# A hybrid attention layer: gates as one silu in place on ScalarE, multiplied in on GpSimd chunk by chunk

## The chip, the cores and the metric

One core of a Trainium2 chip runs one launch of the kernel. The metric is device time in microseconds, the median of several executions. TensorE is called PE below, VectorE DVE, ScalarE ACT, GpSimd POOL; SP issues most DMAs.

## The reference

One decoder layer with 512 tokens and a model width of 1024, in f32. The input is normalized and projected to queries, keys, values and gates of two attentions with 8 heads of 64 each: sliding-window attention (window 128, with sinks) and block attention (a query sees its own block of 256, causally, and the past one). Each attention's output is multiplied by silu(gate) before the output projection; a gated per-layer embedding and a last norm follow.

```python
a_out = swa_attention(a_q, a_k, a_v, sinks, rel_bias[:, :8])
b_out = moba_attention(b_q, b_k, b_v, rel_bias[:, 8:])
mixed = jnp.concatenate([a_out * jax.nn.silu(a_g), b_out * jax.nn.silu(b_g)], axis=-1)
x = x + mixed @ w_out
gate = jax.nn.sigmoid(rms_norm(x, ple_g) @ w_ple_gate)
return rms_norm(x + (p_i @ w_ple_proj) * gate, final_norm)
```

## The kernel before

Every f32 product on PE is made of three products of high and low halves, so a result that PE needs again is split: ACT copies it to the high half (`split_T`, L143) and DVE subtracts to get the low half (L144). Activations and gates lie transposed, as 8 chunks of 128 channels by 512 tokens: `O[c]` is attention output, `G[c]` the raw gate; chunks 0 to 3 belong to the window attention, 4 to 7 to the block attention, two heads to a chunk.

The middle phase interleaves two things on PE, in an order written by hand. One is a stream of projection pieces (L451 to L453 and L137 to L139), whose results ACT and DVE evacuate: queries (`make_q`, L498, L499), keys (`make_k`, L143, L144, followed by a POOL DMA, L508), values, and raw gates (`raw_g`, L527; the last gate by DVE, L529). The other is attention steps. `swa_step(u)` runs 16 window steps: scores on PE (L551), DVE adds the bias and takes the row's minimum of the negated scores (L554), ACT takes the exponential with its row sum (L557), POOL folds two halves (L563), DVE normalizes by the reciprocal (L564, L566); one step later PE transposes the rows (L574), ACT and DVE split the transpose (`pta`, L143, L144), POOL masks it (L582); another step later PE multiplies by the values (L591), and ACT and DVE evacuate to `O` (L596, L601). `moba_step(m)` does the same for the block attention, 32 steps and 6 to drain: scores L611, reduction L612, exponential L614, normalization L617 to L621, transposes L631 (those of a head run while the next head's scores are taken, so they come some four steps after its exponentials), split `pt` (L143, L144), products with the values L641, one step after the transposes, evacuation L648, L649.

PE and SP keep the order of the program text (`manual_schedule`). On ACT, DVE and POOL a planner orders the instructions by its own estimates of when each can start, so an instruction can run earlier or later than where it is written. A wait for the engine's turn is then in order: what stands behind a waiting instruction on its engine waits too.

The gates: `silu_gate(c)` takes a temporary tile `sg` (two buffers of pool `xa`, shared with the evacuations' `aux`), ACT writes Sigmoid(G) (L534), DVE multiplies by G (L535), POOL multiplies O by it (L536). It is called for chunks 0 to 3 after the last window step, for 4 and 5 at step 33 of the block attention, for 6 and 7 at the split of `O` into `acts`, which feeds the output projection (L137 to L139 with `hi_wo`, `lo_wo`). Where an exponential follows a Sigmoid, or a Sigmoid an exponential, the built kernel has an ACT_TABLE_LOAD between them on ACT.

Of the kernel before, what the change touches and what calls it, by code (L numbers as in the profile page):

```python
# [10 lines left out]
F32 = mybir.dt.float32  # L11
BF16 = mybir.dt.bfloat16
F32R = mybir.dt.float32r
AF = mybir.ActivationFunctionType
ALU = mybir.AluOpType

P = 128
SEQ = 512
# [20 lines left out]
def hybrid_layer_kernel(  # L39
# [16 lines left out]
    nc = tc.nc  # L56
# [22 lines left out]
    def bank(shape, name, tag):  # L79
        return psum.tile(shape, F32, name=name, tag=tag)  # L80
# [60 lines left out]
    def split_T(hi, lo, src):  # L141

        nc.scalar.activation(hi, src, AF.Copy)  # L143
        nc.vector.tensor_sub(lo, src, hi.bitcast(F32))  # L144
# [241 lines left out]
    with ExitStack() as ph2:  # L386
        def pool(name, bufs):
            return ph2.enter_context(tc.tile_pool(name=name, bufs=bufs, reuse_waits="tile"))
# [8 lines left out]
        xa = pool("xa", 2)  # L397

        O = [op.tile([P, SEQ], F32, name=f"O_{c}") for c in range(8)]
        G = {}  # L400
# [3 lines left out]
        def toep(head, swa):  # L404

            if swa:
                b = bp.tile([P, 2, 256], F32, name="b_a", tag="b")
                src = bass.AP(tensor=d_tab.tensor, offset=d_tab.offset + head * JT + JB,
                              ap=[[1, P], [JT, 2], [1, 256]])
            else:  # L410
                b = bp.tile([P, 512], F32, name="b_b", tag="b")
                src = bass.AP(tensor=d_tab.tensor, offset=d_tab.offset + (HA + head) * JT,
                              ap=[[1, P], [1, 512]])
            nc.sync.dma_start(b, src)
            return b
# [16 lines left out]
        def run(n):  # L432
            while stream and (n > 0 or stream[0][0] == 0):
                c, f = stream.popleft()
                n -= c
                f()

        def run_all():
            while stream:
                stream.popleft()[1]()  # L440
# [89 lines left out]
            G[c] = g  # L530

        def silu_gate(c):
            sg = xa.tile([P, SEQ], F32, name="sg", tag="aux")
            nc.scalar.activation(sg, G[c], AF.Sigmoid)  # L534
            nc.vector.tensor_mul(sg, sg, G[c])  # L535
            nc.gpsimd.tensor_mul(O[c], O[c], sg)  # L536


        def swa_scores(c, i, q, kt, bias):
# [63 lines left out]
        def moba_scores(h, i, q, kt, bias):  # L603
            w = (i + 1) * P
            S = bank([P, 512], "Sb", "S")
            st = sp.tile([P, 520], F32, name="stb", tag="st")
            nm = small.tile([P, 1], F32, name="nmb")
            sm = small.tile([P, 1], F32, name="smb")
            ri = small.tile([P, 1], F32, name="rib")
            for j in range(2):  # L610
                nc.tensor.matmul(S[:, :w], q[:, i, :], kt[:, j, :w], start=j == 0, stop=j == 1)  # L611
            nc.vector.tensor_tensor_reduce(st[:, :w], S[:, :w], bias[:, 512 - w:], -1.0, 1.0e38,  # L612
                                           ALU.add, ALU.min, nm)
            nc.scalar.activation(st[:, :w], st[:, :w], AF.Exp, bias=nm, scale=-1.0, accum_out=sm)  # L614

            def norm():
                nc.vector.reciprocal(ri, sm)  # L617
                if i == 3:
                    nc.scalar.activation(st[:, :w], st[:, :w], AF.Copy, scale=ri)
                else:  # L620
                    nc.vector.tensor_scalar_mul(st[:, :w], st[:, :w], ri)  # L621
            return st, norm
# [3 lines left out]
        def moba_trans(g, sts):  # L626
            tp = bank([P, 512], "tpb", "tp")
            o = 0
            for j in GRP[g]:
                for i in range(j, NT):  # L630
                    nc.tensor.transpose(tp[:, o:o + P], sts[i][:, tok(j)], rev)  # L631
                    o += P
            pt = pp.tile([P, 2, 512], F32R, name="pt", tag="pt")
            return lambda: split_T(pt[:, 0, :o], pt[:, 1, :o], tp[:, :o]), pt

        def moba_av(h, g, pt, oacc):
            o = 0
            for j in GRP[g]:
                w = SEQ - j * P
                for l in range(2):  # L640
                    nc.tensor.matmul(oacc[:, j * P:], Vb[:, j, h].rearrange("p a d -> p (a d)"),  # L641
                                     pt[:, l, o:o + w], start=j == 0 and l == 0, stop=j == 3 and l == 1)
                o += w

        def moba_evac(h, oacc):
            c, s = 4 + h // 2, h % 2
            aux = xa.tile([DH, 512], F32, name="auxb", tag="aux")
            nc.scalar.activation(aux, oacc[DH:P, :], AF.Copy)  # L648
            nc.vector.tensor_add(O[c][s * DH:(s + 1) * DH, :], oacc[0:DH, :], aux)  # L649
# [97 lines left out]
        swa_step(16)  # L747
        swa_step(16)
        for c in range(4):
            silu_gate(c)  # L750
        run(12)


# [4 lines left out]
        def moba_step(m):  # L758
            h, i = divmod(m, 4)
            norm = None  # L760
            if h < HB:
                if i == 0 and h + 2 < HB:
                    bb[h + 2] = toep(h + 2, False)
                st, norm = moba_scores(h, i, qb[h // 2][h % 2], kb[h // 2][h % 2], bb[h])
                sts[h, i] = st
            pace(per * 0.4)
            if norm:
                norm()
            new = None
            if h > 0 and i > 0 and h - 1 < HB:  # L770
                sp_, pt = moba_trans(i - 1, [sts[h - 1, k] for k in range(NT)])
                sp_()
                new = (h - 1, i - 1, pt)
            pace(per * 0.4)
            if ptq:
                h2, g2, pt2 = ptq.popleft()
                if g2 == 0:
                    ob[h2] = bank([P, 512], "oaccb", "o")
                moba_av(h2, g2, pt2, ob[h2])
                if g2 == 2:  # L780
                    moba_evac(h2, ob[h2])
            if new:
                ptq.append(new)
            pace(per * 0.2)

        for m in range(32):
            moba_step(m)
        per = 2.0
        for m in range(32, 38):
            moba_step(m)  # L790
            if m == 33:
                for c in (4, 5):
                    silu_gate(c)
        run_all()

        for c in range(KC):
            if c >= 6:
                silu_gate(c)
            split_T(acts[:, c, 0, :], acts[:, c, 1, :], O[c])

# [190 lines left out]
```

## Time and profile before

| | |
|---|---|
| median of 3 runs | 323.25 us (322.18 to 323.43) |
| profiled execution | 322.3 us, span 320.6 us |
| PE busy | 307.7 us, 96% |
| DVE busy | 226.0 us, 70% |
| ACT busy | 185.9 us, 58% |
| POOL busy | 66.3 us, 21% |
| middle phase with attention | about 32 to 220 us |

Times in rows are counted from the span's start. A timeline row gives the start, the duration, the engine, the line and operation, the tiles, and in brackets the idle time of the engine before it with what ended it. PE's matmuls are pipelined, so their durations overlap.

### The profile page before, as it was taken

The page shows a single profiled execution, that of the slowest core. Times are in us where ns is not written, and L with a number is a line of the kernel's source. Part 1 is how long each engine was busy: PE and PEld are TensorE (multiplying, and loading weights), DVE is VectorE, ACT ScalarE, POOL GpSimd, SP SyncE. Part 2 cuts the span into 40 slices and gives each one's busy share as a digit, 9 for nine tenths or more (in the row PEclk, how much of TensorE's full clock was granted, in tenths as well). Part 3 has the DMA queues.
Part 4 walks back from the last instruction along what each step waited for, and adds up shares of the span by engine and source line. Part 5 has one row for each costly group of instructions (what it writes and reads, how often), then busy time and mean ns, then how long its engine had stood idle before and what let it go on. Part 6 is the DMA issues. An engine that isn't in the chain of part 4 may idle for free.

```text
span 320.6 us, 4721 instructions
## 1 busy us (share of the span) xinstructions
PE 307.7 (96%) x1641; PEld 259.9 (81%) x1641; DVE 226.0 (70%) x516; ACT 185.9 (58%) x419; POOL 66.3 (21%) x118
## 2 busy tenths in 40 slices
PE   7999999999999999899999999999999999999990
PEld 6878788888889888699888878877888888888890
DVE  2876766886787868878878796859758656672544
ACT  4755656656475648677678676788157323541341
POOL 1240102435434351600003130012300110000011
PEclk9999999999999999999999999999999999999997
DMA  7962598150405072751443403004956700000113
GB/s 234 390 164 83 148 227 232 41 133 1 127 7 177 23 183 76 200 155 40 135 98 120 112 0 133 1 0 116 384 174 246 264 1 0 2 0 0 66 67 131
DMA packets 33224, 37.61 MB, mean 117 GB/s; under 512 B 1432, under 2 KB 24992, under 8 KB 33200
## 3 DMA queue, kind: packets, MB, share of 16 engines
q1 hardware_dynamic: 31952, 33.94, 34.0%
q0 software_dynamic: 800, 2.62, 4.2%
q10 hardware_dynamic: 448, 0.74, 0.7%
q8 instruction: 13, 0.21, 0.3%
q14 instruction: 11, 0.09, 0.1%
HBM read 32.52 MB, written 2.16 MB: 108 GB/s over the span
## 4 chain that ended last, share of the span: by engine, by line
PE 72%; DVE 12%; issue 6%; ACT 4%; POOL 3%; DMA 1%; POOLq 0%; SPq 0%; ACTq 0%; DVEq 0%
PE acc L451 8%; PE acc L452 8%; PE acc L453 8%; PE acc L137 7%; PE acc L139 7%; PE acc L138 7%; PE acc_ple L283 3%; PE acc_akv L302 3%; PE Sb L611 3%; PE accv L137 2%; PE oaccb L641 2%; PE accv L139 2%; PE accv L138 2%; PE tpb L631 2%; DVE q L499 2%
## 5 line engine op out<-in xcount | busy, mean ns | idle before, releaser
L557 ACT ACTIVATE st<-st,nm 128x257 f32<-128x257 f32 (+1 forms) x32 | 15.2, 478 | 22.0 <-DVE nm L554 20.0
L137 PE MATMUL acc<-hi_wg,h 128*128 128x512 f32 (+1 forms) x72 | 26.7, 370 | 0.0
L139 PE MATMUL acc<-hi_wg,h 128*128 128x512 f32 (+1 forms) x72 | 26.4, 367 | 0.0
L451 PE MATMUL acc<-acts,hi_bkq 128*128 128x512 f32 x64 | 26.4, 412 | 0.0
L138 PE MATMUL acc<-lo_wg,h 128*128 128x512 f32 (+1 forms) x72 | 26.3, 365 | 0.0
L451 PE MATMUL acc<-acts,hi_aqg 128*128 128x512 f32 x64 | 26.2, 410 | 0.0
L137 PE MATMUL acc<-hi_wo,acts 128*128 128x512 f32 x64 | 25.4, 397 | 0.5 <-DVE G L529 0.5
L453 PE MATMUL acc<-acts,lo_aqg 128*128 128x512 f32 x64 | 25.2, 393 | 0.0
L453 PE MATMUL acc<-acts,lo_bkq 128*128 128x512 f32 x64 | 25.1, 392 | 0.0
L139 PE MATMUL acc<-hi_wo,acts 128*128 128x512 f32 x64 | 25.1, 392 | 0.0
L452 PE MATMUL acc<-acts,hi_bkq 128*128 128x512 f32 x64 | 25.1, 392 | 0.0
L138 PE MATMUL acc<-lo_wo,acts 128*128 128x512 f32 x64 | 25.1, 392 | 0.0
L452 PE MATMUL acc<-acts,hi_aqg 128*128 128x512 f32 x64 | 25.1, 392 | 0.0
L614 ACT ACTIVATE stb<-stb,nmb 128x128 f32<-128x128 f32 (+3 forms) x32 | 17.8, 558 | 9.0 <-DVE nmb L612 8.7
L582 POOL TENSOR_SCALAR_AFFINE_SELECT pta<-pta 128x512 fp32r<-128x512 f32 x24 | 17.3, 719 | 14.3 <-DVE pta L144 13.2
L137 PE MATMUL accv<-hi_bv,acts 128*128 128x256 f32 x64 | 18.7, 293 | 1.5 <-DVE kt L144 1.5
L536 POOL TENSOR_TENSOR O<-O,sg 128x512 f32<-128x512 f32 x8 | 11.4, 1428 | 39.5 <-DVE sg L535 39.3
L139 PE MATMUL accv<-hi_bv,acts 128*128 128x256 f32 x64 | 18.0, 282 | 0.0
L138 PE MATMUL accv<-lo_bv,acts 128*128 128x256 f32 x64 | 18.0, 281 | 0.0
L839 ACT ACTIVATE sq<-x 128x512 f32<-128x512 f32 x15 | 9.5, 631 | 14.2 <-DVE x L901 11.6
L612 DVE CUSTOM_DVE_ANT_0 stb<-Sb,b_b 128x128 f32<-128x128 f32 (+3 forms) x32 | 15.5, 485 | 2.4 <-PE Sb L611 2.3
L508 POOL DMA_DIRECT2D kt<-kt x10 | 5.6, 563 | 51.1 <-DVE kt L144 48.7
(167 smaller groups left out, 872.6 us busy)
## 6 DMA issues: line engine op xcount, KB each, us to landing
raw_aqg<-in_w_in_dram SPq DMA_DIRECT2D x8, 512.0 KB, 5.3
raw_bkq<-in_w_in_dram SPq DMA_DIRECT2D x8, 512.0 KB, 4.6
raw_wo<-in_w_out_dram SPq DMA_DIRECT2D x4, 1024.0 KB, 6.3
raw_wg<-in_w_ple_gate_dram SPq DMA_DIRECT2D x4, 1024.0 KB, 5.0
kt<-kt POOLq DMA_DIRECT2D x10, 256.0 KB, 4.0
x_t<-in_x_dram SPq DMA_DIRECT2D x4, 512.0 KB, 7.4
raw_bv<-in_w_in_dram SPq DMA_DIRECT2D x2, 1024.0 KB, 5.4
b_b<-d_tab SPq DMA_DIRECT2D x8, 256.0 KB, 4.6
```

Source lines behind the costliest of these rows:

```text
L137: nc.tensor.matmul(acc, sh, mh, start=first, stop=False)
L138: nc.tensor.matmul(acc, sh, ml, start=False, stop=False)
L139: nc.tensor.matmul(acc, sl, mh, start=False, stop=last)
L283: nc.tensor.matmul(pacc[t, n], (pTl if j == 1 else pTh)[:, k, tok(t)], (wpl if j == 2 else wph)[:, n, k], start=k == 0 and j == 0, stop=k ...
L451: nc.tensor.matmul(acc, w.hi[:, k, cs], acts[:, k, 0, :], start=k == 0, stop=False)
L452: nc.tensor.matmul(acc, w.hi[:, k, cs], acts[:, k, 1, :], start=False, stop=False)
L453: nc.tensor.matmul(acc, w.lo[:, k, cs], acts[:, k, 0, :], start=False, stop=k == KC - 1)
L536: nc.gpsimd.tensor_mul(O[c], O[c], sg)
L557: nc.scalar.activation(st[:, s, lo_k:257], st[:, s, lo_k:257], AF.Exp, bias=nm[:, s:s + 1], scale=-1.0, accum_out=sm[:, s:s + 1])
L582: nc.gpsimd.affine_select(out=pt[:, :, b, :].rearrange("p j (s q) -> p j s q", s=2), in_=pt[:, :, 1, :].rearrange("p j (s q) -> p j s q", ...
L612: nc.vector.tensor_tensor_reduce(st[:, :w], S[:, :w], bias[:, 512 - w:], -1.0, 1.0e38, ALU.add, ALU.min, nm)
L614: nc.scalar.activation(st[:, :w], st[:, :w], AF.Exp, bias=nm, scale=-1.0, accum_out=sm)
```

## The change

Sigmoid and two products become one Silu on ACT, in place in `G[c]`, and one product `O[c] * G[c]`, on POOL for chunks 0 to 5 and on DVE for 6 and 7. The temporary tile is gone. In the text, the four window gates' silu stays where `silu_gate` was called, and their products are written after block steps 1, 4, 7 and 10.

```diff
         def silu_gate(c):
-            sg = xa.tile([P, SEQ], F32, name="sg", tag="aux")
-            nc.scalar.activation(sg, G[c], AF.Sigmoid)
-            nc.vector.tensor_mul(sg, sg, G[c])
-            nc.gpsimd.tensor_mul(O[c], O[c], sg)
+            (nc.vector if c >= 6 else nc.gpsimd).tensor_mul(O[c], O[c], G[c])
+
+        def silu(c):
+            nc.scalar.activation(G[c], G[c], AF.Silu)
...
         swa_step(16)
         swa_step(16)
         for c in range(4):
-            silu_gate(c)
+            silu(c)
         run(12)
...
         for m in range(32):
             moba_step(m)
+            if m in (1, 4, 7, 10):
+                silu_gate((m - 1) // 3)
         per = 2.0
         for m in range(32, 38):
             moba_step(m)
             if m == 33:
                 for c in (4, 5):
+                    silu(c)
                     silu_gate(c)
         run_all()
...
         for c in range(KC):
             if c >= 6:
+                silu(c)
                 silu_gate(c)
             split_T(acts[:, c, 0, :], acts[:, c, 1, :], O[c])
```

In the changed kernel the Silu is line L536 and its product L533. The planner moves them. On ACT, in the window attention, between the splits of a projection weight (L116) and the exponentials of step 1 (`G_593` is chunk 0's gate):

```order
 L527 ACTIVATE G_593<-acc 128x512
 L116 ACTIVATE hi_aqg_615<-raw_aqg_431 128x512 x3
+L536 ACT_TABLE_LOAD
+L536 ACTIVATE G_593<-G_593 128x512
+L557 ACT_TABLE_LOAD
 L557 ACTIVATE st,sm<-st,nm 128x257 x2
 L143 ACTIVATE pta<-tp_626 128x256
```

A load, the Silu and a load back now stand ahead of the exponentials. The same three rows come for chunk 1 ahead of step 5's exponentials, chunk 2 ahead of step 8's, chunk 3 ahead of step 12's and chunk 4 ahead of a 128x384 exponential (L614) of the block attention's seventh head, each soon after its gate was written.

On DVE, in window step 8, before and now (L564 and L566 x2 normalize step 8, `pta` is the split of step 7's transpose, L554 x2 of width 256 are step 9's reductions):

```order
L554 ISA nm 128x1
L118 TENSOR_TENSOR lo_bv_957<-raw_bv_744,hi_bv_956 128x512
L564 RECIPROCAL ri<-sm 128x2
L566 TENSOR_SCALAR st<-st,ri 128x128 x2
L144 TENSOR_TENSOR pta<-tp_980,pta 128x256
L554 ISA st,nm<-S,b_a,nsink 128x256
```

```order
L554 ISA nm 128x1
L118 TENSOR_TENSOR lo_bv_957<-raw_bv_744,hi_bv_956 128x512
L554 ISA st,nm<-S,b_a,nsink 128x256
L554 ISA nm 128x1
L564 RECIPROCAL ri<-sm 128x2
L144 TENSOR_TENSOR pta<-tp_980,pta 128x256
L566 TENSOR_SCALAR st<-st,ri 128x128 x2
```

The normalization of step 8 now stands behind a reduction of step 9 and behind the split of step 7.

On ACT, at the end of the block attention's scores, before and now (`G_2365` and `G_2468` are the gates of chunks 4 before and 5 now; `hi_wo` is a split of the output projection's weight, L614 at 128x512 the last exponential, L619 its normalization):

```order
L143 ACTIVATE pt<-tpb 128x384
L116 ACTIVATE hi_wo_2502<-raw_wo_2244 128x512
L143 ACTIVATE pt<-tpb 128x384
L614 ACTIVATE stb,smb<-stb,nmb 128x512
L619 ACTIVATE stb<-stb,rib 128x512
L648 ACTIVATE auxb<-oaccb 64x512
L534 ACT_TABLE_LOAD
L534 ACTIVATE sg<-G_2365 128x512
L143 ACTIVATE pt<-tpb 128x512
```

```order
L143 ACTIVATE pt<-tpb 128x384
L536 ACT_TABLE_LOAD
L536 ACTIVATE G_2468<-G_2468 128x512
L614 ACT_TABLE_LOAD
L614 ACTIVATE stb,smb<-stb,nmb 128x512
L143 ACTIVATE pt<-tpb 128x384
L619 ACTIVATE stb<-stb,rib 128x512
L116 ACTIVATE hi_wo_2494<-raw_wo_2236 128x512
L648 ACTIVATE auxb<-oaccb 64x512
L527 ACTIVATE G_2557<-acc 128x512
L143 ACTIVATE pt<-tpb 128x512
L536 ACT_TABLE_LOAD
```

The second `pt` split of 128x384 stood ahead of the last exponential and now stands behind two loads, a Silu and that exponential; the load and Sigmoid that stood ahead of the 128x512 split are gone, and a load for the next Silu follows it.

## Rows read from the trace of the kernel before

**Rows 1.** The page's part 1: busy us, share of the span, instructions of each engine.

```profile
PE 307.7 (96%) x1641; PEld 259.9 (81%) x1641; DVE 226.0 (70%) x516; ACT 185.9 (58%) x419; POOL 66.3 (21%) x118
```

**Rows 2.** PE's waits: tile and line <- releaser: us in total, times, longest.

```profile
PE accv L137 <- DVE kt L144: 1.5, 1, 1.5
...
PE tp L574 <- DVE st L566: 0.6, 2, 0.3
PE oaccb L641 <- DVE pt L144: 0.6, 2, 0.4
PE acc L137 <- DVE G L529: 0.5, 1, 0.5
```

**Rows 3.** Busy time by stretch: PE, PEld, DVE, ACT, POOL, PEclk, DMA share, GB/s.

```profile
130.00:134.00 4.00, 2.48 (x14) 1.86 (x13) 3.79 (x4) 3.47 (x6) 3.25 (x5) 1.00 0.73 200
```

**Rows 4.** ACT's groups: count | busy, mean ns | idle before, releaser.

```profile
L899 ACT ACTIVATE sg<-acc 128x512 f32<-128x512 f32 x7 | 4.2, 596 | 8.1 <-PE acc L139 8.1
...
L534 ACT ACT_TABLE_LOAD x2 | 2.6, 1283 | 0.0
...
L188 ACT ACT_TABLE_LOAD x1 | 1.3, 1283 | 2.3 <-issue 2.3
```

**Rows 5.** Timeline of ACT from 211 us.

```profile
211.83 1.28 ACT L534 ACT_TABLE_LOAD   x1
213.13 0.63 ACT L534 ACTIVATE sg<-G 128x512 f32<-128x512 f32 x1
```

**Rows 6.** The gates' products, by line: ns min/median/max, first and last start.

```profile
L535 DVE TENSOR_TENSOR sg<-sg,G x8: 682/836/1784, 126.4 to 224.3; 128x512 f32<-128x512 f32 x8
...
L536 POOL TENSOR_TENSOR O<-O,sg x8: 1274/1290/1673, 127.2 to 226.2; 128x512 f32<-128x512 f32 x8
```

**Rows 7.** Timeline of ACT, DVE and PE at window step 1.

```profile
50.20 0.51 ACT L557 ACTIVATE st<-st,nm 128x257 f32<-128x257 f32 x1 [0.19 <-DVE nm L554]
...
52.35 0.48 DVE L566 TENSOR_SCALAR st<-st,ri 128x128 f32<-128x128 f32 x2 [0.23 <-POOL st L563]
...
54.37 0.38 PE L574 MATMUL tp<-rev,st 128*128 128x128 f32 x2
```

**Rows 8.** Timeline of ACT at window steps 5 and 12, their first exponentials.

```profile
67.16 0.51 ACT L557 ACTIVATE st<-st,nm 128x257 f32<-128x257 f32 x1 [2.02 <-POOL pta L582]
...
100.17 0.41 ACT L557 ACTIVATE st<-st,nm 128x129 f32<-128x129 f32 x1 [2.77 <-DVE nm L554]
```

**Rows 9.** Timeline of ACT, DVE and PE at window step 8.

```profile
82.53 0.40 ACT L557 ACTIVATE st<-st,nm 128x129 f32<-128x129 f32 x1 [2.09 <-DVE nm L554]
...
83.65 0.48 DVE L566 TENSOR_SCALAR st<-st,ri 128x128 f32<-128x128 f32 x2
84.05 0.42 DVE L144 TENSOR_TENSOR pta<-tp,pta 128x256 fp32r<-128x256 f32 x1
...
84.23 0.38 PE L574 MATMUL tp<-rev,st 128*128 128x128 f32 x2
```

**Rows 10.** Timeline of DVE after the window steps.

```profile
129.54 3.03 DVE L535 TENSOR_TENSOR sg<-sg,G 128x512 f32<-128x512 f32 x2 [1.25 <-ACT sg L534]
```

**Rows 11.** Timeline of ACT, DVE and PE in the block attention's seventh head.

```profile
196.15 0.62 ACT L614 ACTIVATE stb<-stb,nmb 128x384 f32<-128x384 f32 x1 [0.64 <-DVE nmb L612]
...
197.42 0.55 DVE L144 TENSOR_TENSOR pt<-tpb,pt 128x384 fp32r<-128x384 f32 x1
...
199.71 0.51 PE L641 MATMUL oaccb<-pt,Vb 128*128 128x384 f32 x2
```

**Rows 12.** The same timelines in its eighth head.

```profile
208.40 0.49 ACT L143 ACTIVATE pt<-tpb 128x384 fp32r<-128x384 f32 x1 [0.57 <-PE tpb L631]
208.86 0.72 ACT L614 ACTIVATE stb<-stb,nmb 128x512 f32<-128x512 f32 x1
...
209.35 0.55 DVE L144 TENSOR_TENSOR pt<-tpb,pt 128x384 fp32r<-128x384 f32 x1
...
210.61 0.57 PE L641 MATMUL oaccb<-pt,Vb 128*128 128x256 f32 x4
```

## Prediction

> **What bounds the kernel now.** I read the busy line of the page first [rows 1]: PE is busy for 307.7 of 320.6 us, 96%, ACT for 58%, GpSimd for 21%. PE's instructions and their order are the same in both kernels (the order is written by hand, and so is SP's), so the time changes only by what PE waits for. Second, the list of PE's waits [rows 2]: 1.5 us once for the DVE half of a k split, 0.6 us for softmax rows to be transposed, 0.6 us for a split transpose, 0.5 us for the DVE copy of the last gate. That is nearly all that a change off PE can give back; what it can cost is not limited so. Third, the timeline at each place where the order of ACT or DVE changes: how long before PE needs it does a result arrive (the slack), and how much later will it arrive now.
>
> The profiled execution took 322.3 us, 0.95 below the median of the three runs, 323.25. Its rows give differences, which I add to the median.
>
> **The price of one gate.** Before, ACT switched tables for the gates twice: one load ahead of four Sigmoids at 124 us, one back, and one ahead of the last four. The order of the changed kernel has 15 loads in place of 4. The planner puts each silu of chunks 0 to 5 next to the place where its G is written, ahead of an exponential, so that each of the six has a load before and one after. A load is 1.28 us [rows 4]. Silu itself has no row; Sigmoid on the same tile took 0.63 [rows 5], and I take that (nothing and 0.72, a 128x512 exponential [rows 12], are the ends; that moves a gate by under 0.7). A detour is 1.28 + 0.63 + 1.28 = 3.2 us in which ACT serves nobody. What follows a load starts 0.02 us after it ends [rows 5]. The Trainium skill (ScalarE: Activation LUTs, What ACT_TABLE_LOAD costs) adds a drain to each switch and counts about 2.66 us; the rows show no such drain, and by the page a detour would be 6.0 us (rival 4).
>
> **Chunk 0**, ahead of the exponentials of window step 1. ACT idled 0.19 us before the exponential at 50.20, so this moves by 3.2 - 0.2 = 3.0. Its rows were normalized at 52.83, and PE transposed them at 54.37: 1.5 of slack [rows 7]. PE waits 3.0 - 1.5 = **+1.5** (0 to 3.0).
> **Chunk 1**, ahead of step 5: 2.02 us of idle time stand before that exponential [rows 8], so it moves by 1.2. The slack to the transposes is like that of step 1, about 1.5. **+0.2** (0 to 1.2).
> **Chunk 2**, ahead of step 8: idle 2.09, moved by 1.1, but the rows were ready at 84.13 for a transpose at 84.23, slack 0.1 [rows 9]. DVE's order also puts the previous step's split (0.42) and one score reduction ahead of the two normalizing products; the reduction fits into the wait, the split does not: 1.1 - 0.1 + 0.4 and a hand-over is 1.6. The 0.6 that PE waited for softmax rows two steps later [rows 2] then falls into this wait: **+1.1** (0 to 1.7).
> **Chunk 3**, ahead of step 12: idle 2.77 [rows 8], moved 0.4, some slack: **+0.2** (0 to 0.4).
> **Chunk 4**, in block attention. Exponentials there have a whole head of time, since a head is transposed while the next is scored, so they don't matter; the split of a transpose, one step from its product, does. The split stands behind the delayed 128x384 exponential: 3.2 - 0.64 idle = 2.6 later. DVE's half ended at 197.97 for a product at 199.71, slack 1.7 [rows 11]: **+0.9** (0 to 2.6).
> **Chunk 5**: the detour and the 0.72 exponential go ahead of a split that started at 208.40 after 0.57 idle; a 0.6 weight split moves behind it. 3.2 + 0.7 - 0.6 - 0.6 = 2.7 later. DVE's half ended at 209.90 for products from 210.61 [rows 12]; the second product, 0.1 later, is the first that needs it: slack 0.8, so PE waits 2.7 - 0.8: **+1.9** (0 to 2.7).
> **Chunks 6, 7**: one load, no return, and their product on DVE costs 0.68, as the fastest row of the old product [rows 6]; the acts of these chunks come no later than now, and PE has no wait for them in its list [rows 2]: 0. The exchange of Sigmoid's table later falls into the 8.1 us in which ACT waited for PE before those Sigmoids [rows 4]: 0.
>
> **What is removed.** DVE loses eight products. The two at 129.54 took 3.03 us, and the k split queued behind them is the one PE waited 1.5 us for [rows 2, 10]. They are gone from there, and so are ACT's Sigmoids and GpSimd's 1.3 us products: **-1.5** (0 to -1.5). In the tail one load and one Sigmoid at 211.83 stood ahead of a split; they now stand behind it: **-0.5** of the 0.6 for split transposes. The last gate's copy comes earlier since GpSimd's products no longer run beside DVE there, but behind the 1.9: **-0.3** of 0.5.
>
> **GpSimd.** Its order has the products of chunks 0 to 3 among the window steps and after them, earlier than the text of the program; one took 1.29 us [rows 6], on a queue that is 21% busy. I take 0, since most of DVE's work in those steps reads PSUM, which GpSimd doesn't. Ends: 0 and 1.1 each (rival 3).
>
> Sum: 1.5 + 0.2 + 1.1 + 0.2 + 0.9 + 1.9 - 1.5 - 0.5 - 0.3 = **+3.5 us**, so 323.25 + 3.5 = **326.75 us**, in round numbers **326.7**. PE's clock stood at 1.00 in the stretch with the 1.5 us wait [rows 3], so waits of this length bring no clock term.
>
> **Rivals.** A measurement of this kernel can tell some 0.5%, 1.6 us, from no change.
> 1. **Slack covers every detour**, and only the gains stay: 323.25 - 2.3 = 321.0, faster. It decides at chunks 0, 2 and 5: DVE, freed of products, would have to hand over 1.5 to 2 us earlier than now. For it: ACT is 58% busy. Against: DVE's products are not gone from the places where the detours stand, but from 126 to 133 us. 0.09.
> 2. **Costs and gains nearly cancel**: each of the four large waits is 0.5 to 0.8 us shorter than reckoned, since the two engines catch up while PE waits: 322.5 to 324.8. 0.20.
> 3. **GpSimd's products block DVE.** The old DVE product took 0.68 alone and 1.78 beside GpSimd [rows 6], 1.1 us more. If the three products among window steps and the two of chunks 4 and 5 each cost DVE that much where it is late anyway, three of them are seen by PE: 326.7 + 3.3 = 330.0. The Trainium skill (SBUF — State Buffer, Who interferes with whom) calls this an exclusive lock between the two engines, taken by operations with two SBUF inputs; the slow rows agree. Against: in the window steps most of DVE's work reads PSUM. 0.09.
> 4. **A load costs more than its row.** The first load of the run is preceded by 2.3 us that nothing explains [rows 4]; were that part of each load, six detours would grow by 4.6 each: 326.7 + 27.6 = 354. By the page's drain it would be 2.8 each, 343.5. Against it, the 0.02 us above. 0.02.
>
> **How the numbers follow.** The forecast with its bounds, 324.9 to 329, has 0.60. Slower by over 0.5% is the forecast, rivals 3 and 4: 0.71; within 0.5% rival 2: 0.20; faster rival 1: 0.09. The range leaves out rivals 1 and 4 and half of rival 3: 321.6 to 330.2.
>
> **What would show it.** In the changed profile ACT has 15 loads of 1.28 us; PE waits of 1 to 2 us appear before the transposes of window steps 1 and 8 (for DVE's normalized rows) and before products in block attention for the split of a transpose (twice); the 1.5 us wait at the first v product is gone; PE's busy time is unchanged. It is wrong if those four waits are absent, or if DVE's products in the window steps grow beside GpSimd's.

## The result and the profile after

The changed kernel takes 327.45 us (median of 4, 325.23 to 328.39) against 323.34 for the kernel before (median of 4, 322.18 to 324.16): ratio 1.0118, 95% interval 1.0076 to 1.016. It is slower by 4.1 us; 326.7 was predicted, in a range of 321.6 to 330.2. The profiled execution took 328.0 us, with a span of 326.3.

The page's busy line answers to [rows 1] (busy us, share, instructions):

```profile
PE 311.2 (95%) x1641; PEld 262.0 (80%) x1641; DVE 218.1 (67%) x510; ACT 199.5 (61%) x430; POOL 62.7 (19%) x116
```

PE has the same 1641 instructions and 3.5 us more of busy time; the prediction had it unchanged. PE's waits (us in total, times, longest) answer to [rows 2]:

```profile
PE tp L574 <- DVE st L566: 3.1, 3, 1.7
...
PE oaccb L641 <- ACT pt L143: 1.0, 1, 1.0
...
PE oaccb L641 <- DVE pt L144: 0.9, 3, 0.4
PE accv L137 <- DVE q L499: 0.4, 1, 0.4
```

The 1.5 us for the k split and the 0.5 us for the last gate are gone; 3.1 us for softmax rows and 1.0 us for a split transpose are new. ACT's groups answer to [rows 4] (count | busy, mean ns | idle before):

```profile
L536 ACT ACT_TABLE_LOAD x7 | 9.0, 1283 | 0.1
L557 ACT ACT_TABLE_LOAD x4 | 5.1, 1283 | 0.1
L536 ACT ACTIVATE G<-G 128x512 f32<-128x512 f32 x8 | 5.0, 631 | 0.1
L614 ACT ACT_TABLE_LOAD x2 | 2.6, 1283 | 0.0
```

With one load each at L188 and L903 these are the 15 loads. The timeline at window step 1, as [rows 7]:

```profile
51.63 1.28 ACT L536 ACT_TABLE_LOAD   x1
...
52.93 0.63 ACT L536 ACTIVATE G<-G 128x512 f32<-128x512 f32 x1
53.58 1.28 ACT L557 ACT_TABLE_LOAD   x1
...
54.87 0.51 ACT L557 ACTIVATE st<-st,nm 128x257 f32<-128x257 f32 x1
...
57.25 0.49 PE L574 MATMUL tp<-rev,st 128*128 128x128 f32 x2 [1.12 <-DVE st L566]
```

The detour lasts 54.87 - 51.63 = 3.24 us, and PE waits 1.12 before the transposes. At window step 8, as [rows 9]:

```profile
83.67 1.28 ACT L536 ACT_TABLE_LOAD   x1
...
86.91 0.41 ACT L557 ACTIVATE st<-st,nm 128x129 f32<-128x129 f32 x1
...
87.82 0.17 DVE L564 RECIPROCAL ri<-sm 128x2 f32<-128x2 f32 x1 [0.98 <-ACT st L557]
88.23 0.42 DVE L144 TENSOR_TENSOR pta<-tp,pta 128x256 fp32r<-128x256 f32 x1 [0.24 <-ACT pta L143]
...
88.57 0.87 DVE L566 TENSOR_SCALAR st<-st,ri 128x128 f32<-128x128 f32 x2
...
89.00 0.30 PE L574 MATMUL tp<-rev,st 128*128 128x128 f32 x1 [1.65 <-DVE st L566]
...
89.59 0.30 PE L574 MATMUL tp<-rev,st 128*128 128x128 f32 x1 [0.29 <-DVE st L566]
```

PE waits 1.65 and 0.29 us here, as DVE normalizes late and behind the previous step's split. What follows is in the busy time by stretch (columns as [rows 3], PEclk in the third place from the end):

```profile
88.00:90.00 2.00, 0.71 (x4) 0.53 (x5) 1.74 (x6) 1.24 (x5) 1.20 (x2) 1.00 1.04 302
90.00:92.00 2.00, 2.00 (x8) 1.63 (x7) 1.39 (x5) 1.39 (x4) 0.94 (x3) 0.63 0.76 182
92.00:94.00 2.00, 2.00 (x9) 1.71 (x8) 1.59 (x4) 0.59 (x1) 0.00 (x0) 0.52 0.00 0
94.00:96.00 2.00, 2.00 (x13) 1.69 (x13) 1.08 (x5) 0.89 (x3) 1.29 (x1) 1.00 0.00 0
```

Before 90 us PE had been busy for 0.71 of 2 us; then the granted clock falls to about half (1.2 in place of 2.4 GHz) for some 3.4 us, and 8 or 9 matmuls run in a stretch that later holds 13. The kernel before has no stretch at half clock outside its last microseconds. The half clock is some 1.5 of the 3.5 us of PE's added busy time (by the table below). Most of the rest lies in the first 14 us, ahead of the change: from 10 to 12 us this execution ran 6 matmuls, the kernel before 11. In the other profiled execution of the changed kernel, told below, PE is busy for 308.3 us.

In block attention, chunk 4's detour delays both halves of a split. PE's own wait is short, and the weight loads (PEld) ahead of its two matmuls wait 0.47 and 0.56:

```profile
204.45 0.19 PEld L641 LDWEIGHTS oaccb<-pt,Vb 128*128 128x128 f32 x1 [0.47 <-ACT pt L143]
...
205.19 0.19 PEld L641 LDWEIGHTS oaccb<-pt,Vb 128*128 128x128 f32 x1 [0.56 <-DVE pt L144]
205.19 0.44 PE L641 MATMUL oaccb<-pt,Vb 128*128 128x384 f32 x1 [0.30 <-DVE pt L144]
```

Chunk 5's detour ends in a wait for ACT's half of the split, as foreseen:

```profile
216.00 0.72 ACT L614 ACTIVATE stb<-stb,nmb 128x512 f32<-128x512 f32 x1
...
216.72 0.47 ACT L143 ACTIVATE pt<-tpb 128x384 fp32r<-128x384 f32 x1
...
217.24 0.38 PE L641 MATMUL oaccb<-pt,Vb 128*128 128x256 f32 x1 [1.02 <-ACT pt L143]
```

### The profile page after: what moved, and what is told of

Same layout as the page of the kernel before. It is cut to its first block, busy times and chain, and to the rows that moved or that the text cites. A ratio compares the mean times of both kernels' runs of the same rounds, so it can differ in the third digit from the quotient of the medians.

```text
span 326.3 us, 4722 instructions
## 1 busy us (share of the span) xinstructions
PE 311.2 (95%) x1641; PEld 262.0 (80%) x1641; DVE 218.1 (67%) x510; ACT 199.5 (61%) x430; POOL 62.7 (19%) x116
## 4 chain that ended last, share of the span: by engine, by line
PE 72%; ACT 11%; DVE 7%; issue 6%; POOL 1%; DMA 1%; POOLq 0%; ACTq 0%
PE acc L451 8%; PE acc L452 8%; PE acc L453 8%; PE acc L137 7%; PE acc L139 7%; PE acc L138 7%; PE acc_ple L283 4%; PE acc_akv L302 3%; PE accv L137 2%; PE oaccb L641 2%; PE accv L139 2%; PE accv L138 2%; PE Sb L611 2%; PE oacc L591 2%; PE S L551 2%
## 5 line engine op out<-in xcount | busy, mean ns | idle before, releaser
L451 PE MATMUL acc<-acts,hi_aqg 128*128 128x512 f32 x64 | 26.6, 415 | 0.0
L452 PE MATMUL acc<-acts,hi_aqg 128*128 128x512 f32 x64 | 25.5, 399 | 0.0
L614 ACT ACTIVATE stb<-stb,nmb 128x128 f32<-128x128 f32 (+3 forms) x32 | 17.8, 557 | 8.0 <-DVE nmb L612 7.9
L641 PE MATMUL oaccb<-pt,Vb 128*128 128x512 f32 (+3 forms) x64 | 15.2, 329 | 2.1 <-ACT pt L143 1.0
```

What stands on the lines that cost most here:

```text
L451: nc.tensor.matmul(acc, w.hi[:, k, cs], acts[:, k, 0, :], start=k == 0, stop=False)
L452: nc.tensor.matmul(acc, w.hi[:, k, cs], acts[:, k, 1, :], start=False, stop=False)
```

## Where the time goes, place by place

PE's 1641 matmuls have one order in all kernels here. So I took the start of each in a trace, less its start in the trace of before, both counted from the first matmul; what this difference gains or loses between two places is what that stretch of the program costs. Up to 50.7 us of the kernel before, where nothing was changed, single executions differ by -0.3 to +2.0 us (after: +1.6, all of it in the first 14 us); this is left out. "After" is the profiled execution of 328.0 us; the other columns are experiments, told below.

| stretch of before, us | predicted | after | after again | Exp everywhere | Silu late |
|---|---|---|---|---|---|
| chunk 0, 50.7 to 56.3 | +1.5 | +1.39 | +1.38 | 0 | 0 |
| chunk 1, to 80.6 | +0.2 | -0.03 | -0.02 | +0.12 | 0 |
| chunk 2, to 97.0 | +1.1 | +2.91 | +1.37 | +0.18 | +0.02 |
| chunk 3, to 128.4 | +0.2 | -0.01 | -0.01 | -0.01 | -0.01 |
| k split, to 140.5 | -1.5 | -1.32 | -1.32 | -1.32 | -1.36 |
| chunk 4, to 204.2 | +0.9 | +0.90 | +0.90 | 0 | 0 |
| chunk 5, to 213.4 | +1.9 | +1.75 | +1.77 | 0 | 0 |
| tail, to 230.3 | -0.8 | -1.49 | -1.48 | -1.70 | -1.02 |
| all, to the end | +3.5 | +4.1 | +2.6 | -2.7 | -2.4 |

## Experiments

Theory A: the loads around each hoisted Silu, and the half clock behind the longest wait, cost the time. Rival B: GpSimd's products among the window steps, or DVE's new order. Each time is compared with runs of the kernel before on the same chip.

**Exp in place of Silu.** The gate's function is changed, not its place.

```diff
-            nc.scalar.activation(G[c], G[c], AF.Silu)
+            nc.scalar.activation(G[c], G[c], AF.Exp)
```

> The gate's function is Exp in place of Silu, so the output is gated by another function; the rest of the changed kernel stays, each function in the same place in ACT's order, without the loads around it. Theory A (the loads around each gate make the waits): ACT has 2 table loads less than the kernel before or fewer, the waits of 1.1 and 1.65 us before the transposes of window steps 1 and 8 are gone, the clock does not drop, and the time is that of the kernel before less the gains of 1.5 to 2.3 us, 321 to 322. Rival B (GpSimd's products among the window steps hold DVE up, or the new order on DVE): these are the same here, so about 327.

319.88 us, ratio 0.9894 (0.9862 to 0.9927). PE's waits:

```profile
PE tp L574 <- DVE st L566: 0.6, 2, 0.4
PE accv L137 <- DVE q L499: 0.4, 1, 0.4
PE oaccb L641 <- DVE pt L144: 0.4, 1, 0.4
```

The new waits are gone and GpSimd's products are all there, so the waits come with the loads. But without the loads DVE's order at window step 8 is the old one again (both products of the normalization, then the split), so this run does not part the loads from DVE's new order there; the quarter Silu below does so in part. The time is a microsecond below what A expected, since the removed work is worth 3.0 us here (1.32 and 1.70 in the table), not 2.3.

**GpSimd's products left out** for chunks 0 to 5.

```diff
-            (nc.vector if c >= 6 else nc.gpsimd).tensor_mul(O[c], O[c], G[c])
+            if c >= 6: nc.vector.tensor_mul(O[c], O[c], G[c])
```

> The GpSimd products of chunks 0 to 5 are left out, so six of the eight chunks stay ungated; the Silus, their loads and their places stay. Theory A: 326.5 to 328, the waits of 1.1 and 1.65 us at window steps 1 and 8 as in the changed kernel, and the clock drop after the second. Rival B (GpSimd's products hold DVE up): 324 or less, the waits shorter by about 1 us each.

326.26 us (324.58 to 328.02), ratio 1.0101 (1.0049 to 1.0153). Against before its profile loses +1.39 at chunk 0, +2.91 at chunk 2, +1.77 at chunk 5, 4.15 in all: the changed kernel's figures to 0.05 us. The median is a little under what A gave: two of the four executions, at a mean clock of 0.993 and 0.994, took 324.6 and 324.8 us, and two at 0.988 took 327.8 and 328.0. (The mean clock is the granted share of the full clock over an execution.) PE's wait list has the same waits for softmax rows:

```profile
PE tp L574 <- DVE st L566: 3.0, 3, 1.6
```

and the busy time by stretch has the same half clock after step 8, in this profiled execution (328.02 us):

```profile
90.00:92.00 2.00, 2.00 (x6) 1.55 (x5) 1.38 (x5) 1.38 (x4) 0.93 (x3) 0.50 0.79 189
92.00:94.00 2.00, 2.00 (x10) 1.78 (x9) 1.19 (x3) 0.59 (x1) 0.00 (x0) 0.65 0.00 0
```

Rival B has fallen for GpSimd's products.

**The changed kernel again.**

> The changed kernel once more, for the share of its executions in which the clock drops. Theory A (a wait of 1.65 us at window step 8, and in some executions half clock behind it): two groups of executions, those with a mean clock of 0.988 to 0.990 at 327 to 328.4 and those at 0.993 or more near 325, 2 us or more apart; more than a third of them in the first. Rival D (the lower mean clock has another cause and costs nothing by itself): the times of the two groups overlap.

326.07 us, ratio 1.009 (1.0063 to 1.0117). Of all ten executions of this kernel, six had a mean clock of 0.987 to 0.989 and took 326.8 to 328.4 us; four had 0.994 or 0.995 and took 325.1 to 325.3. The groups do not overlap; their means are 2.2 us apart, their nearest members 1.5. The profiled execution this time is one of the four (325.08). PE's timeline has the same waits:

```profile
87.61 0.30 PE L574 MATMUL tp<-rev,st 128*128 128x128 f32 x1 [1.65 <-DVE st L566]
88.21 0.30 PE L574 MATMUL tp<-rev,st 128*128 128x128 f32 x1 [0.29 <-DVE st L566]
```

and the busy time by stretch full clock after them, though PE was busy for only 0.69 of the 2 us around the waits:

```profile
86.60:88.60 2.00, 0.69 (x4) 0.51 (x5) 1.73 (x7) 1.24 (x5) 1.19 (x2) 1.00 1.03 302
88.00:90.00 2.00, 1.79 (x10) 1.56 (x11) 1.64 (x6) 1.43 (x4) 1.27 (x3) 1.00 1.15 290
90.00:92.00 2.00, 2.00 (x14) 1.79 (x13) 1.65 (x4) 0.63 (x2) 0.24 (x1) 1.00 0.03 7
```

So two traces of one program differ at chunk 2 by 2.91 - 1.37 = 1.54 us: the price of the half clock. Everywhere else they agree to 0.02 us from 50.7 us on. The rest of the 2.9 us between these two executions, 1.4, lies ahead of the first changed instruction.

**Exp for chunk 2 alone.**

```diff
-            nc.scalar.activation(G[c], G[c], AF.Silu)
+            nc.scalar.activation(G[c], G[c], AF.Exp if c == 2 else AF.Silu)
```

> The changed kernel with Exp in place of Silu for chunk 2 alone, so that this chunk is gated by another function and has no loads around it. Theory A: the wait of 1.65 us at window step 8 is gone and with it the stretch of half clock behind it (some 1.7 us); 0.6 us of waits for softmax rows come back: 324 to 325, mean clock 0.993 or 0.994. Rival D (the clock drop has nothing to do with that wait): the drop stays, somewhere, and the time is 325.7 to 326.5 with a mean clock of 0.989.

324.03 us, ratio 1.0036 (1.0013 to 1.0059); all ten mean clocks lie between 0.992 and 0.997. Chunk 2's stretch costs 0.11 in place of 2.91 and no other stretch changes by more than 0.03. In PE's list the wait of 1.1 at chunk 0 is the longest that is left for softmax rows:

```profile
PE tp L574 <- DVE st L566: 1.8, 3, 1.1
```

So there is no wait at step 8 and no drop. DVE's order there is the old one again too.

**Silu on chunk 2 alone**, Exp on the others, and the same with the Silu on 128 of 512 columns.

```diff
-            nc.scalar.activation(G[c], G[c], AF.Silu)
+            nc.scalar.activation(G[c], G[c], AF.Exp if c != 2 else AF.Silu)
```

> The changed kernel with Exp in place of Silu for all chunks but chunk 2, so seven chunks are gated by another function; only chunk 2 has loads around its Silu. Theory A (that wait by itself brings the clock down): 1.3 us of net wait at window step 8 on top of the 319.9 of the kernel with Exp everywhere, and in some executions half clock behind it: 321.2 without the drop, about 323 with it. Rival D (the drop needs the earlier wait of chunk 0, or something else of the changed kernel): 321.2 in all executions, no stretch at half clock before the tail.

> As the run with Silu on chunk 2 alone, but the Silu takes 128 of the 512 columns and the rest of that chunk's gate stays raw: the detour is some 0.45 us shorter, and DVE's order at window step 8 is again that of the kernel before (normalizing products ahead of the previous step's split). Theory A (the wait there is detour less idle time and slack, plus the split in front): 2.8 - 2.1 - 0.1, a wait of 0.6 us or less in place of 1.65, no drop, 320 to 320.5. Rival E (any pair of loads ahead of these exponentials brings wait and drop): a wait over 1.2 us, 321.2 to 323.

321.09 us (ratio 0.995, 0.9929 to 0.9971) and 318.98 us (0.9886, 0.9855 to 0.9916). PE's timeline at the transposes of step 8, with the whole Silu:

```profile
85.42 0.30 PE L574 MATMUL tp<-rev,st 128*128 128x128 f32 x1 [1.35 <-DVE st L566]
```

and with the quarter:

```profile
84.65 0.49 PE L574 MATMUL tp<-rev,st 128*128 128x128 f32 x2 [0.49 <-DVE st L566]
```

With the whole one, nine of ten executions took 320.0 to 321.9 us at 0.993 to 0.997; one took 322.64 at 0.989. That one was not profiled. Its clock is what a stretch at half clock would give, but no trace shows the drop without chunk 0's detour, so rival D is not settled. With the quarter, DVE's order is the old one and the wait 0.49, within what A gave; four executions, none below 0.992. The quarter also tells what DVE's order adds:

```profile
84.02 0.17 DVE L564 RECIPROCAL ri<-sm 128x2 f32<-128x2 f32 x1 [0.92 <-ACT st L557]
```

From DVE's reciprocal to PE's transpose it takes 84.65 - 84.02 = 0.63 us in the old order, and 89.00 - 87.82 = 1.18 in the changed kernel. So, as an estimate, some 0.55 of the wait of 1.65, and the 0.29 behind it, are DVE's new order, and the rest is ACT's detour. In every run here that order comes only with the loads around a whole Silu. The quarter's time is lower than expected by a microsecond, again the removed work (1.32 and 1.67).

**Silu late**: the kernel before, with Silu into the temporary tile and no DVE product.

```diff
             sg = xa.tile([P, SEQ], F32, name="sg", tag="aux")
-            nc.scalar.activation(sg, G[c], AF.Sigmoid)
-            nc.vector.tensor_mul(sg, sg, G[c])
+            nc.scalar.activation(sg, G[c], AF.Silu)
             nc.gpsimd.tensor_mul(O[c], O[c], sg)
```

> The kernel before with Silu written to the temporary tile in place of Sigmoid, and without DVE's product: the gates stay batched where they were, with 4 table loads or one or two more, and GpSimd multiplies O by the temporary tile. Theory A: only the gains of the change are left, the 1.5 us wait for the k split is gone or halved, 321.5 to 322.5. Rival C (the two DVE products cost nothing on the path, and the wait for the k split comes from elsewhere): as before, 323.3.

320.63 us, ratio 0.9928 (0.9901 to 0.9955): **faster than both kernels**. The Silus stay where they were written, with 5 loads in all. That it is the temporary tile, whose two buffers are also the evacuations', that keeps them there is argued, and was not tested by itself. The k split's wait is gone from PE's list, as in the changed kernel, and the query split's is there:

```profile
PE accv L137 <- DVE q L499: 0.4, 1, 0.4
```

The time is 0.9 below what A gave; the tail, of which A does not speak, gains 1.02.

**Silu late, products of chunks 6 and 7 on DVE** (the edit is against the run above).

```diff
-            nc.gpsimd.tensor_mul(O[c], O[c], sg)
+            (nc.vector if c >= 6 else nc.gpsimd).tensor_mul(O[c], O[c], sg)
```

> The kernel with Silu into the temporary tile at the old places, with the products of chunks 6 and 7 on DVE as in the changed kernel. Theory A: the wait for the last gate's copy before the output projection goes, as in the changed kernel's tail, some 0.3 to 0.7 us: 320.0 to 320.4 beside 320.6. Rival: the products of chunks 6 and 7 are off the path in that kernel, 320.6, no difference.

320.93 us, ratio 0.994 (0.9915 to 0.9965), no better: a miss. In its trace the tail gains 1.01 us, 1.02 without this edit; GpSimd's last two products are off the path.

**No load for the gates: Tanh.** The kernel before is edited. With h = x/2, silu(x) = h(1 + tanh h); the raw gates are evacuated with a factor of one half (not in the diff).

```diff
-            nc.scalar.activation(sg, G[c], AF.Sigmoid)
-            nc.vector.tensor_mul(sg, sg, G[c])
+            nc.scalar.activation(sg, G[c], AF.Tanh)
+            nc.vector.scalar_tensor_tensor(sg, sg, 1.0, G[c], op0=ALU.add, op1=ALU.mult)
```

> The kernel before with silu(x) as h + h*tanh(h), h = x/2: the raw gates are evacuated with a factor of one half, Tanh in place of Sigmoid, DVE's product as (t + 1)*h, GpSimd's product as before. The built kernel has no table load for it, since Tanh needs none beside Exp. Theory A (loads and DVE's products are separate terms): the loads of the kernel before stood in idle time, so only the tail's load is saved, 0.5 us or less, and the wait of 1.5 us for the k split stays: 322.5 to 323.3. Rival F (the 1.5 us wait came from the load and the Sigmoids on ACT, not from DVE's products): 321 to 321.7, that wait gone or under 0.5.

321.91 us, ratio 0.9963 (0.994 to 0.9985). In PE's list of waits the one for the k split stays:

```profile
PE accv L137 <- DVE kt L144: 1.3, 1, 1.3
```

DVE's products are there and the load is not, and the wait stays; in the late Silu the loads are there and those products are not, and it is gone. So the 1.5 us came from DVE's products: rival F falls. The time is 0.6 below A's lower end, since the tail without its load gains 1.16 us, not 0.5. The trace has two loads, at L188 and L899. The Trainium skill (ScalarE: Activation LUTs, Table sets) lists tanh in the set of exp, and the trace agrees: no load stands between Tanh and the exponentials.

**Tanh in the changed kernel's places**, with GpSimd's O*h first and DVE's (t + 1)*O after; the raw gates are halved as above.

```diff
-            (nc.vector if c >= 6 else nc.gpsimd).tensor_mul(O[c], O[c], G[c])
+            nc.vector.scalar_tensor_tensor(O[c], G[c], 1.0, O[c], op0=ALU.add, op1=ALU.mult)
...
-            nc.scalar.activation(G[c], G[c], AF.Silu)
+            (nc.vector if c >= 6 else nc.gpsimd).tensor_mul(O[c], O[c], G[c])
+            nc.scalar.activation(G[c], G[c], AF.Tanh)
```

> Silu as h*(1 + tanh(h)) with h = x/2 in the changed kernel's places: GpSimd multiplies O by h (DVE for chunks 6 and 7), Tanh goes in place on ACT without loads, DVE multiplies (t + 1) into O, by the planner's order for the window gates partly after the k split that PE waited for. Theory A: no load, no detour, waits at window steps 1 and 8 gone, DVE's late product of chunk 3 still ahead of the k split of 1.5 us (0.7 instead of 3.0 us of DVE work, so a wait of 0 to 0.7): 320.5 to 321.5, between the late Silu's 320.6 and the batched Tanh's 321.9. Rival B (products spread over the window steps hold DVE up): 322 or more, with waits for DVE at these steps.

322.03 us, ratio 0.9953 (0.9935 to 0.9971), above what A gave. The k split's stretch gains 1.32 as hoped, but between 56.3 and 80.6 us 1.14 are lost, and 0.43 more between 97.0 and 128.4, which was not followed up. The timeline of POOL, DVE and PE in the first of these:

```profile
75.92 1.02 POOL L583 TENSOR_SCALAR_AFFINE_SELECT pta<-pta 128x512 fp32r<-128x512 f32 x1 [1.48 <-DVE pta L144]
76.91 0.73 POOL L564 TENSOR_TENSOR st<-st 128x256 f32<-128x256 f32 x1
...
77.67 0.83 DVE L567 TENSOR_SCALAR st<-st,ri 128x128 f32<-128x128 f32 x2 [1.11 <-POOL st L564]
78.46 0.49 PE L575 MATMUL tp<-rev,st 128*128 128x128 f32 x2 [0.88 <-DVE st L567]
```

The planner put GpSimd's mask, which waits for DVE's split, ahead of the fold that DVE's normalization needs, and PE waits 0.88. So B's mechanism exists, in another kernel: products added among the window steps can reorder a queue that PE waits for. In the changed kernel the same stretch (chunk 1) cost nothing.

## Why the prediction was right, step by step

The sign and the mechanism came as told, and so did three of the four waits; the fourth, chunk 4's, is only 0.30 us on PE itself and costs 0.90 with its weight loads. By the table the terms came to +4.1, or +2.6 in the execution without the half clock, against +3.5. That the sum lies between the two is in part luck: it missed 1.54 us of half clock and 0.7 us of gain in the tail, errors of opposite sign, and how near the median comes depends on how many executions have the half clock (+4.1 us where by mean clock three of four have it, +2.9 where three of six have it).

- **The price of a gate**: 3.2 us told, 3.24 measured, Silu 0.63. By the page on ScalarE's drain (the Trainium skill, ScalarE: Activation LUTs, What ACT_TABLE_LOAD costs) a detour would be 6.0, an estimate from its 2.66 us a switch. Here ACT starts the next instruction 0.01 to 0.02 us after a load, and the trace disagrees with the drain. Rival 4 is out.
- **Chunks 0, 1, 3, 4, 5**: +1.5, 0.2, 0.2, 0.9, 1.9 told; +1.39, 0, 0, 0.90, 1.75 measured. Idle time ahead of the exponential, then slack to the matmul, gave each cost within 0.2 us. Chunk 0's wait itself is 1.12 of its 1.39.
- **Chunk 2**: a first wait of 1.6 told, 1.65 measured; less the 0.6 that it swallows, +1.1 told (1.6 - 0.6 is 1.0). A second wait of 0.29, from a normalization that took 0.87 instead of 0.48 [rows 9], makes it +1.37. That matched. **The step that failed is the last one of the sum, "waits of this length bring no clock term"**: [rows 3] showed one wait of 1.5 us with the clock at 1.00, and I took it for all waits near that length. Here it cost 1.54 us more in the profiled execution, and going by the mean clock in six of ten.
- **The k split**: -1.5 told. The stretch up to the product gained 1.75, and the query split next in line (`q`, L499) brought a new wait of 0.42: -1.32.
- **The tail**: -0.8 told, -1.49 measured, mis-sized. I took the gain from PE's own waits in [rows 2]. The weight loads ahead of those matmuls waited as well, in the kernel before 0.54, 0.51 and 0.89 us:

```profile
215.16 0.19 PEld L641 LDWEIGHTS oaccb<-pt,Vb 128*128 128x128 f32 x1 [0.54 <-DVE pt L144]
219.44 0.41 PEld L641 LDWEIGHTS oaccb<-pt,Vb 128*128 128x128 f32 x3 [0.51 <-DVE pt L144]
223.28 0.19 PEld L137 LDWEIGHTS acc<-hi_wo,acts 128*128 128x128 f32 x1 [0.89 <-DVE G L529]
```

 The three places gave back 0.43, 0.49 and 0.57.
- **GpSimd at zero, rival 3**: right, by the run without its products.
- **Rivals 1 and 2**: the detours were not covered, and rival 2's shorter waits did not come; without the half clock the kernel would still be some 2 us slower, as its four executions at full clock are: 325.2, only 0.4 above the range of rival 2, but with waits as long as reckoned.

## What to carry to other kernels

When an activation from another table set becomes free to move (in place, no shared buffer that orders it), look in the built order for how many loads it brings: here a batch of four gates behind one load became four pairs of loads. Price each pair as load + function + load, less the idle time ahead of it, less the slack to the matmul that needs what stands behind it. And where a new wait of more than a microsecond falls on PE, keep a second price for the clock behind it.

## What the runs showed that was not expected

- One program with the same waits (1.65 and 0.29 us) kept full clock in one profiled execution and ran some 3.4 us at half clock in another, 1.54 us longer. Which of the two comes was not settled. Four profiles have loads around a whole Silu at chunk 2. The two with the drop had the longer first 14 us (+1.6 us each against the kernel before), the two without had +0.2 and -0.3. Four traces are only a hint, but it fits that the two groups of executions lie 2.2 us apart where the half clock alone is 1.54.
- Waits of 1.12, 1.35 and 1.5 us were followed by full clock in every profile here.
- A pair of DVE normalizations beside GpSimd's mask took 0.87 us in the changed kernel at step 8 and 0.83 in the kernel with Tanh in place, against 0.48 at step 8 in the kernel before. It did so too with GpSimd's products left out, where the second wait is again 0.29. Such slow ones are not new: in the kernel before one such normalization takes 0.29 us in the median and up to 0.68, but none of the slow ones stands at step 8.
- The first 14 us, the same in all kernels, vary by up to 2.3 us between profiled executions. That is more than most terms of the sum; only a comparison by place separates them.
